# An opening and a last layer norm rebuilt in a two-layer encoder kernel: transfers in whole rows, a product on four column groups, rows of the last tile in PSUM

## The chip, the cores and the metric

The kernel runs on one core of a Trainium2 chip. The metric is the device time of one execution in microseconds (us), the median of several runs; less is better. The profile comes from one more execution, recorded by the hardware profiler.

## The reference, cut to what matters

256 tokens of width 1024 go through two layers. Each layer is a mixer (two kinds of heads side by side, one input projection, one output projection), a layer norm, a mixture of 16 experts with two experts for a token, and a second layer norm. All data is float32.

```python
def reference(x, ...):
    for i in range(2):
        mix = _even_mixer(x, ...) if i == 0 else _odd_mixer(x, ...)
        x = _layer_norm(ALPHA * x + mix, ln1_g[i], ln1_b[i])
        ffn = _hier_moe(x, ...)
        x = _layer_norm(ALPHA * x + ffn, ln2_g[i], ln2_b[i])
    return x

def _layer_norm(x, g, b):
    mu = mean(x); var = mean((x - mu) ** 2)
    return (x - mu) * rsqrt(var + 1e-5) * g + b

def _even_mixer(x, w_in, ...):
    h = x @ w_in
    z, xbc, dt_raw, q, k, v = split(h)
    dt = softplus(dt_raw + dt_bias)
...
```

## The kernel before, in words

One builder writes the instructions of all engines; the order of the program text is the order on each engine, and nothing is reordered. Weights come in pieces of 1 MB (128 partitions by 8 KB) into a ring of 19 buffers (`w`). `fill` (L163) issues their DMAs on SP's queue as soon as buffers come free.

**Opening** (`mixer0`, L305). Five small DMAs come first on SP's queue: `wdt` (the 16 columns of the first weight that give dt, 64 KB) and the transposed input `xT` in four pieces of 256 KB (rows of 2 KB in each partition). `load_constants` (L245) then issues the first weight buffer in two halves (rows of 4 KB), a second one, and constants (`pp`, `cc`, `cm`) between further weights. x is held as two float32r parts: ACT makes the high part `xh` (L319), DVE the rest `xl` (L320), in four pieces. PE meanwhile makes dt's product `dtp` (L339): eight matmuls of 16 columns from `xT` as it is, each recorded as two passes.

The main product of layer 0 goes over 32 pieces of 128 columns (loop at L548). `presplit` splits a piece of weights into high and low part (`split`, L222: ACT at L230, DVE at L231; tile `pair`), two pieces ahead. `mm3_stationary` (L234) then issues 8 matmuls high by `xh` (L238), 8 high by `xl` (L240) and 8 low by `xh` (L242). After a piece the convolution (L390, L393) or a copy takes its result off PSUM.

**Router constants.** After piece 14 the loop calls `router_prep(0)` (L843): six DVE operations add up the router's weights times the norm's gains (tile `rsum`, L852 to L855), one PE matmul (L857) adds over the partitions into `rbp`, and two DVE operations make `rbias` and the weights from it (L859, L860). For layer 1 `moe` (L863) calls it in its third quarter.

**End of a layer.** `moe` yields twice near its end; the code that follows takes it on with `next(moe)` (`mixer1` L1388 and L1389, `finale` L790). `combine` (L1082) adds an expert quarter into the PSUM banks `acc` of a token tile; the very last one is a float32 matmul of 512 columns (L1089). `residual_half` (L733) makes `xres` = ALPHA x + acc, `statistics` (L740) its sums, `moments` (L743) mean and a first root (two small ACT operations, L748 and L749), `factor` (L751) one Newton step on columns of 128x1 (L754 to L756), `shift` (L761) minus mean times factor.

`finale` writes the output. Tile 0 is scaled by ACT (L766) and gets gain and offset from POOL (L806, L807; stored from SP's queue, L808). Tile 1 is done by DVE: subtract the mean and times gain (L797), times factor plus offset (L799), a half at a time, second half first; L797 of the first of them stands ahead of `factor`. Its stores are issued from ACT's queue (L800). The gains and offsets `gb` lie in SBUF, as does `xres`.

Of the kernel before, what the change touches and what calls it, by code (L numbers as in the profile page):

```python
# [92 lines left out]
class Builder:  # L93
# [69 lines left out]
    def fill(self, n=1000, parts=1):  # L163
        while n and self.loaded < len(self.seq) and self.free > self.keep:
# [6 lines left out]
            for i in range(parts):  # L171
                cs = slice(n_el * i // parts, n_el * (i + 1) // parts)
                self.nc.sync.dma_start(w[:rows, cs], src[:, cs])
# [60 lines left out]
    def mm3_stationary(self, ps, hi, lo, xh, xl, n=8):  # L234

        mm = self.nc.tensor.matmul
        for c in range(n):
            mm(ps, hi[:, c, :], xh[:, c, :], start=(c == 0), stop=False)  # L238
        for c in range(n):
            mm(ps, hi[:, c, :], xl[:, c, :], start=False, stop=False)  # L240
        for c in range(n):
            mm(ps, lo[:, c, :], xh[:, c, :], start=False, stop=(c == n - 1))  # L242


    def load_constants(self):  # L245
        nc = self.nc
        nc.scalar.preload_act_table_set(EXP_LN)
        self.fill(1, 2)
        self.fill(1)
# [55 lines left out]
    def mixer0(self):  # L305
# [36 lines left out]
        dts = [self.T([128, 512], name="dts")]  # L342
        sc.activation(dts[0][:16, :256], dtp[:16, :256], AF.Copy)
# [196 lines left out]
        for i in range(32):  # L540
# [36 lines left out]
            if i == 16:  # L577
                self.reserve(4)
                self.gdone(2)
# [161 lines left out]

    def moments(self, t):
# [47 lines left out]
    def finale(self, gb, out, moe):  # L790
# [4 lines left out]
        def vector(t, s):  # L795
            x, mv = self.xres[:, t, HALVES[s]], self.mv[t]
            v.scalar_tensor_tensor(x, x, mv[:, 0:1], gb[:, 0, HALVES[s]], op0=OP.subtract, op1=OP.mult)  # L797
            yield
            v.scalar_tensor_tensor(x, x, mv[:, 3:4], gb[:, 1, HALVES[s]], op0=OP.mult, op1=OP.add)  # L799
            nc.scalar.dma_start(out[:, t, HALVES[s]], x)  # L800
            yield

# [7 lines left out]
        acc = next(moe)  # L810
        self.residual_half(1, 0, acc, stats=False)
        self.factor(0)
        self.shift(0)
        self.statistics(1, 0)
        self.residual_half(1, 1, acc)
# [992 lines left out]
```

## Time and profile before

| | |
|---|---|
| median of 3 runs | 526.71 us (526.57 to 528.31) |
| the profiled execution: its own time | 526.84 us |
| the profiled execution: span of the core | 525.0 us |
| mean granted TensorE clock | 0.992 |
| PE busy | 497.6 us, 95% |
| DVE, ACT, POOL busy | 301.6, 247.8, 94.1 us |
| DMA | 142.37 MB, mean 271 GB/s |

How to read it: the span runs from the first to the last recorded instruction; the execution's own time has 1.84 us more around it. PE's matmuls overlap one another, so the mean of one can be several times the distance between two. In a row of the timeline the first number is the start, the second the time from the first start to the last end of the instructions in it (x says how many); the bracket behind gives the engine's idle time before it and what ended it. Names such as `ps<-xh,pair` mean output from inputs.

### The profile page before, as it was taken

The page shows a single profiled execution, that of the slowest core. Times are in us where ns is not written, and L with a number is a line of the kernel's source. Part 1 is how long each engine was busy: PE and PEld are TensorE (multiplying, and loading weights), DVE is VectorE, ACT ScalarE, POOL GpSimd, SP SyncE. Part 2 cuts the span into 40 slices and gives each one's busy share as a digit, 9 for nine tenths or more (in the row PEclk, how much of TensorE's full clock was granted, in tenths as well). Part 3 has the DMA queues.
Part 4 walks back from the last instruction along what each step waited for, and adds up shares of the span by engine and source line. Part 5 has one row for each costly group of instructions (what it writes and reads, how often), then busy time and mean ns, then how long its engine had stood idle before and what let it go on. Part 6 is the DMA issues. An engine that isn't in the chain of part 4 may idle for free. (4 is left out here: it accounts for less than half of the span.)

```text
span 525.0 us, 9792 instructions
## 1 busy us (share of the span) xinstructions
PE 497.6 (95%) x3844; PEld 320.7 (61%) x3844; DVE 301.6 (57%) x683; ACT 247.8 (47%) x519; POOL 94.1 (18%) x161
## 2 busy tenths in 40 slices
PE   5999899999999999999999998999999999999990
PEld 2999898989777553433323698788776443533320
DVE  3777757777876762251206774887667741612047
ACT  4787467569783442240215583466644431512041
POOL 0073000120000002240002078910000002600204
PEclk9999999999999999999999999999999999999996
DMA  7999942006277969999979833070469699999602
GB/s 277 420 421 418 389 164 81 1 1 240 82 271 252 419 254 380 424 420 420 418 306 424 346 102 139 4 311 9 162 241 368 279 411 399 424 393 423 273 1 80
DMA packets 21179, 142.37 MB, mean 271 GB/s; under 512 B 2373, under 2 KB 2629, under 8 KB 4741
## 3 DMA queue, kind: packets, MB, share of 16 engines
q1 hardware_dynamic: 20024, 135.67, 64.5%
q0 software_dynamic: 816, 5.51, 2.8%
q8 instruction: 32, 0.52, 0.4%
q10 hardware_dynamic: 288, 0.52, 0.3%
q14 instruction: 19, 0.15, 0.1%
HBM read 140.64 MB, written 1.05 MB: 270 GB/s over the span
## 5 line engine op out<-in xcount | busy, mean ns | idle before, releaser
L1023 PE MATMUL gu<-w,XT 128*32 128x512 f32 x960 | 107.0, 594 | 0.0
L231 DVE TENSOR_TENSOR pair<-w,pair 128x1024 fp32r<-128x1024 f32 x57 | 70.3, 1236 | 25.0 <-ACT pair L230 24.6
L1023 PEld LDWEIGHTS gu<-w,XT 128*32 128x32 f32 x960 | 29.7, 110 | 65.4 <-issue 62.4
L230 ACT ACTIVATE pair<-w 128x1024 fp32r<-128x1024 f32 x57 | 60.2, 1060 | 8.8 <-PE ps L242 4.6
L1053 PE MATMUL dn<-w,hT 128*32 128x512 f32 x512 | 59.5, 596 | 0.9 <-ACT hT L1042 0.9
L1033 DVE TENSOR_TENSOR hd<-sg,gu 128x256 f32<-128x256 f32 x16 | 6.7, 420 | 78.6 <-ACT sg L1031 78.6
L238 PE MATMUL ps<-xh,pair 128*128 128x256 f32 x288 | 42.3, 289 | 1.4 <-ACT pair L230 1.4
L1072 DVE SCALAR_TENSOR_TENSOR pair<-dn,ws,pair 128x512 fp32r<-128x512 f32 x30 | 22.4, 749 | 35.2 <-ACT pair L1066 33.2
L240 PE MATMUL ps<-xl,pair 128*128 128x256 f32 x288 | 39.9, 281 | 0.0
L242 PE MATMUL ps<-xh,pair 128*128 128x256 f32 x288 | 39.8, 280 | 0.0
L1066 ACT ACTIVATE pair<-dn,ws 128x512 fp32r<-128x512 f32 x30 | 20.6, 687 | 37.7 <-PE dn L1053 29.9
L238 PEld LDWEIGHTS ps<-xh,pair 128*128 128x128 f32 x288 | 36.4, 189 | 2.9 <-ACT pair L230 1.9
L242 PEld LDWEIGHTS ps<-xh,pair 128*128 128x128 f32 x288 | 36.6, 188 | 0.0
L240 PEld LDWEIGHTS ps<-xl,pair 128*128 128x128 f32 x288 | 36.5, 188 | 0.0
L780 POOL PARTITION_BROADCAST w<-w x16 | 11.2, 798 | 136.7 <-DMA w<-in_ln_dram 86.5
L1031 ACT ACTIVATE sg<-gu 128x256 f32<-128x256 f32 x16 | 6.1, 381 | 62.5 <-PE gu L1023 62.5
L1053 PEld LDWEIGHTS dn<-w,hT 128*32 128x32 f32 x512 | 14.4, 109 | 30.4 <-issue 25.7
L993 ACT ACTIVATE XT<-gp,pp 128x256 f32<-128x256 f32 x36 | 17.6, 563 | 19.4 <-PE gp L986 19.4
L1549 ACT ACTIVATE pw<-z,sm 128x128 f32<-128x128 f32 (+1 forms) x32 | 13.0, 420 | 22.2 <-DVE sm L1546 9.9
L787 POOL TENSOR_TENSOR xres<-xres,w 128x256 f32<-128x256 f32 (+1 forms) x12 | 16.4, 1369 | 25.4 <-DVE hd L1033 12.7
L160 POOL DMA_DIRECT2D wh<-in_wgu_dram x4 | 2.3, 580 | 100.0 <-PE acc L685 100.0
L301 PE MATMUL vp<-pair,xh 128*128 128x256 f32 x128 | 19.8, 288 | 0.0
(370 smaller groups left out, 954.7 us busy)
## 6 DMA issues: line engine op xcount, KB each, us to landing
w<-in_wgu_dram SPq DMA_DIRECT2D x60, 1024.0 KB, 9.7
w<-in_wd_dram SPq DMA_DIRECT2D x32, 1024.0 KB, 11.3
w<-in_w_dram SPq DMA_DIRECT2D x15, 1024.0 KB, 17.1
w<-in_wout_dram SPq DMA_DIRECT2D x10, 1024.0 KB, 18.4
wh<-in_wgu_dram POOLq DMA_DIRECT2D x4, 1024.0 KB, 7.3
w<-in_wfox_dram SPq DMA_DIRECT2D x4, 1024.0 KB, 15.7
w<-in_wfv_dram SPq DMA_DIRECT2D x2, 1024.0 KB, 5.0
w<-in_wab_dram SPq DMA_DIRECT2D x2, 848.0 KB, 16.8
```

The lines of the kernel that those rows point to most:

```text
L230: self.nc.scalar.activation(vh, src, AF.Copy)
L231: (self.nc.gpsimd if pool else self.nc.vector).tensor_tensor(vl, src, vh.bitcast(F32), op=OP.subtract)
L238: mm(ps, hi[:, c, :], xh[:, c, :], start=(c == 0), stop=False)
L240: mm(ps, hi[:, c, :], xl[:, c, :], start=False, stop=False)
L242: mm(ps, lo[:, c, :], xh[:, c, :], start=False, stop=(c == n - 1))
L301: mm(o, xx[:, 4 * k + c, 128 * t:128 * t + 128], ww[:, c, :], start=(k == 0 and n == 0), stop=(k == 1 and n == 11))
L787: g.tensor_tensor(r, r, gb[:, 0, cs], op=OP.mult)
L993: sc.activation(xt[:, c, :], b[:, i], AF.Identity, bias=bb, scale=g)
L1023: pe.matmul(gu[t][32 * e:32 * e + 32, :], XT[t][:, c, o:o + 32], w[:, e, :], start=(c == 0), stop=(c == 7))
L1053: pe.matmul(b[32 * e:32 * e + 32, :], ht[:, k, 32 * e:32 * e + 32], w[:, e, :], start=(k == 0), stop=(k == 1))
L1066: sc.activation(y, dn[t, s], AF.Copy, scale=WS[t][:, q:q + 1])
L1072: v.scalar_tensor_tensor(yl, b, WS[t][:, q:q + 1], yh.bitcast(F32), op0=OP.mult, op1=OP.subtract)
```

## The change

1. `wdt` is padded to 32 columns for each of its 8 chunks (128 KB) and issued from ACT's queue, ahead of ACT's table load. `xT` comes in one DMA of 1 MB with rows of 8 KB, first on SP's queue. The first weight buffer comes in one DMA as well.
2. A tile of zeros (`idle`, bf16) feeds 8 matmuls of 512 columns ahead of dt's product, and 5 behind it; their result isn't used.
3. ACT makes pieces 0 and 1 of `xh`, DVE pieces 2 and 3, then all of `xl`.
4. dt's eight matmuls go to four groups of 32 columns of the array (partitions 0, 32, 64 and 96 of the output), two in each; a matmul with the constant `fold` later adds the four groups, in the place of two transposes.
5. For the first two pieces, the products with the high part of both stand ahead of those with the low part of both.
6. `router_prep` keeps the DVE sums; the matmul into `rbp` and what follows are `router_sums`, called after piece 16 (layer 0). In layer 1 the sums stand earlier, at the start of the third quarter.
7. In `factor` and `shift` the operations on 128x1 columns with two tensor inputs become TENSOR_SCALAR with one tensor input and two scalars from SBUF columns.
8. In `finale` tile 1's residual is added in place in PSUM; the last combine is two matmuls of 256 columns with an addition behind each; sums, mean and gain are taken from `acc`, and the last step writes to `xres`, which is stored from ACT's queue. `moe` therefore yields four times, in `mixer1` too.

```diff
-            for i in range(parts):
-                cs = slice(n_el * i // parts, n_el * (i + 1) // parts)
-                self.nc.sync.dma_start(w[:rows, cs], src[:, cs])
+            self.nc.sync.dma_start(w[:rows, :n_el], src)
...
         xT = self.G([128, 2048], name="xT")
-        wdt = self.T([128, 8, 16], name="wdt")
-        nc.sync.dma_start(wdt.rearrange("p c n -> p (c n)"), self.a["wdt"])
-        for i in range(4):
-            nc.sync.dma_start(xT[:, i * 512:(i + 1) * 512], self.a["xT"][:, i * 512:(i + 1) * 512])
+        wdt = self.T([128, 8, 32], name="wdt")
+        nc.scalar.dma_start(wdt.rearrange("p c n -> p (c n)"), self.a["wdt"])
+        nc.sync.dma_start(xT, self.a["xT"])
+
+        idle = self.T([128, 512], BF16, name="idle")
+        v.memset(idle, 0.0)
+        wu = self.B("wu")
+        for i in range(8):
+            pe.matmul(wu, idle[:, :128], idle, start=True, stop=True)
         xh = self.G([128, 8, 256], F32R, "xh")
         xl = self.G([128, 8, 256], F32R, "xl")
         xT3 = xT.rearrange("p (c t) -> p c t", c=8)
-        for i in range(4):
-            sc.activation(xh[:, 2 * i:2 * i + 2], xT3[:, 2 * i:2 * i + 2], AF.Copy)
-            v.tensor_sub(xl[:, 2 * i:2 * i + 2], xT3[:, 2 * i:2 * i + 2], xh[:, 2 * i:2 * i + 2].bitcast(F32))
+        chunks = [slice(2 * i, 2 * i + 2) for i in range(4)]
+        for i in (0, 1):
+            sc.activation(xh[:, chunks[i]], xT3[:, chunks[i]], AF.Copy)
+        for i in (2, 3):
+            v.tensor_copy(xh[:, chunks[i]], xT3[:, chunks[i]])
+        for cs in chunks:
+            v.tensor_sub(xl[:, cs], xT3[:, cs], xh[:, cs].bitcast(F32))
         pieces = {}
...
         dtp = self.B("dtp")
         for c in range(8):
-            pe.matmul(dtp[:16, :256], wdt[:, c, :], xT3[:, c, :], start=(c == 0), stop=(c == 7))
+            r = slice(32 * (c % 4), 32 * (c % 4) + 32)
+            pe.matmul(dtp[r, :256], wdt[:, c, :], xT3[:, c, :], start=(c < 4), stop=(c >= 4))
+        for i in range(5):
+            pe.matmul(wu, idle[:, :128], idle, start=True, stop=True)
+        del wu
         presplit(0)
         presplit(1)
...
             for t in range(2):
-                pe.transpose(dtt[:, 16 * t:16 * t + 16], d[:16, 128 * t:128 * t + 128], self.ident[:16, :16])
+                pe.matmul(dtt[:, 32 * t:32 * t + 32], d[:, 128 * t:128 * t + 128], self.cv("fold"), start=True, stop=True)
-            v.tensor_add(dt, dtt[:, :32].rearrange("p (t h) -> p t h", t=2),
+            v.tensor_add(dt, dtt[:, :64].rearrange("p (t h) -> p t h", t=2)[:, :, :16],
...
+            if i == 0:
+
+                ps2 = [self.A("ps")[:, :256] for _ in range(2)]
+                for k in range(2):
+                    self.mm3_stationary(ps2[k], *pieces[k], xh, xl, parts=(0, 1))
             presplit(i + 2)
             hi, lo = pieces.pop(i)
             ps = None
-            if i >= 28:
+            if i < 2:
+                ps = ps2[i]
+                self.mm3_stationary(ps, hi, lo, xh, xl, parts=(2,))
+            elif i >= 28:
...
             if i == 14:
                 self.router_prep(0)
             if i == 16:
+                self.router_sums(0)
                 self.reserve(4)
                 self.gdone(2)
...
-        v.scalar_tensor_tensor(mv[:, 6:7], mv[:, 5:6], mv[:, 5:6], mv[:, 2:3], op0=OP.mult, op1=OP.mult)
+        v.tensor_scalar(mv[:, 6:7], mv[:, 5:6], mv[:, 5:6], mv[:, 2:3], op0=OP.mult, op1=OP.mult)
-        v.tensor_mul(mv[:, 3:4], mv[:, 5:6], mv[:, 6:7])
+        v.tensor_scalar(mv[:, 3:4], mv[:, 6:7], mv[:, 5:6], None, op0=OP.mult)
-        v.scalar_tensor_tensor(mv[:, 4:5], mv[:, 0:1], -1.0, mv[:, 3:4], op0=OP.mult, op1=OP.mult)
+        v.tensor_scalar(mv[:, 4:5], mv[:, 0:1], mv[:, 3:4], -1.0, op0=OP.mult, op1=OP.mult)
...
+        def add(s, cs):
+            a = acc[s][:, cs]
+            v.scalar_tensor_tensor(a, self.xres[:, 1, HALVES[s]][:, cs], ALPHA, a, op0=OP.mult, op1=OP.add)
+
+
+        acc = next(moe)[1]
+        add(0, slice(0, 512))
         self.factor(0)
         self.shift(0)
-        self.statistics(1, 0)
-        self.residual_half(1, 1, acc)
         scalar(0, 0)
         scalar(0, 1)
+        for k in range(2):
+            next(moe)
+            add(1, slice(256 * k, 256 * k + 256))
+        self.st[1] = self.S([128, 2, 6], name="st", bufs=2)
+        for s in range(2):
+            v.bn_stats(self.st[1][:, s, :], acc[s])
         self.moments(1)
-        first = vector(1, 1)
-        next(first)
         self.factor(1)
-        next(first)
-        for _ in vector(1, 0):
-            pass
+        mv = self.mv[1]
+        for s in range(2):
+            a, cs = acc[s], HALVES[s]
+            x = self.xres[:, 1, cs]
+            v.scalar_tensor_tensor(a, a, mv[:, 0:1], gb[:, 0, cs], op0=OP.subtract, op1=OP.mult)
+            v.scalar_tensor_tensor(x, a, mv[:, 3:4], gb[:, 1, cs], op0=OP.mult, op1=OP.add)
+            nc.scalar.dma_start(out[:, 1, cs], x)
...
+    def router_sums(self, layer):
+
+        v, pe = self.nc.vector, self.nc.tensor
+        wr = self.wr
         rbp = self.B("rbp")
-        pe.matmul(rbp[:, :64], self.ones, u[:, :, 0], start=True, stop=True)
+        pe.matmul(rbp[:, :64], self.ones, self.rsum[:, :, 0], start=True, stop=True)
+        del self.rsum
         rbias = self.S([128, 24], name="rbias")
         v.tensor_add(rbias, rbp[:, :24], self.pv("rb", 24 * layer, 24))
...
             if last(q, t, s):
-                pe.matmul(acc[t][s], l.bitcast(F32), yy["last"], start=False, stop=True)
+                for c in (slice(256 * k, 256 * k + 256) for k in parts):
+                    pe.matmul(acc[t][s][:, c], l.bitcast(F32), yy["last"][:, c], start=False, stop=True,
+                              skip_group_check=True)
             else:
                 pe.matmul(acc[t][s], l, yh[:, cs], start=(q == 0), stop=False)
-                pe.matmul(acc[t][s], l, yl[:, cs], start=False, stop=(q == 3))
+                pe.matmul(acc[t][s], l, yl[:, cs], start=False, stop=(q == 3 or (q, t, s) == (2, 1, 1)))
...
         weigh_lo(3, 1, 1)
         combine(3, 1, 0)
-        combine(3, 1, 1)
         yield acc
+        for k in range(2):
+            combine(3, 1, 1, (k,))
+            yield acc
```

The order of the instructions at three places (a row is the line, the operation, output and inputs, the output's size, and in brackets the semaphores that it waits for). ACT's queue in the opening, before:

```order
L247 ACT_TABLE_LOAD
L319 ACTIVATE xh<-xT 128x512 [waits DMAHW1_49]
L319 ACTIVATE xh<-xT 128x512 [waits DMAHW2_49]
L319 ACTIVATE xh<-xT 128x512 [waits DMAHW3_49]
L319 ACTIVATE xh<-xT 128x512 [waits DMAHW4_49]
L230 ACTIVATE pair<-w 128x1024 [waits DMAHW5_49]
L230 ACTIVATE pair<-w 128x1024 [waits DMAHW6_49]
L343 ACTIVATE dts<-dtp 16x256 [waits PE_49]
```

And with the change:

```order
L311 DMA wdt<-in_wdt_dram 128x256
L248 ACT_TABLE_LOAD
L325 ACTIVATE xh<-xT 128x512 [waits DMAHW1_49]
L325 ACTIVATE xh<-xT 128x512
L228 ACTIVATE pair<-w 128x1024 [waits DMAHW2_49]
L228 ACTIVATE pair<-w 128x1024
L356 ACTIVATE dts<-dtp 128x256 [waits PE_49]
L228 ACTIVATE pair<-w 128x1024 [waits DMAHW3_49]
```

`wdt` is now issued here, two of the four splits of x are left, and both halves of the first weight wait for one DMA.

DVE around piece 16, from the last of the router's sums on (L855), before:

```order
L854 TENSOR_TENSOR rsum<-rsum 128x2x64 [waits DVE_49]
L855 TENSOR_TENSOR rsum<-rsum 128x2x32 [waits DVE_49]
L859 TENSOR_TENSOR rbias<-rbp,pp 128x24 [waits PE_49]
L860 SCALAR_TENSOR_TENSOR wrg<-rbp,wrg 128x256
L231 TENSOR_TENSOR pair<-w,pair 128x1024 [waits Activation_49]
L393 SCALAR_TENSOR_TENSOR cy<-ps,pp,cy 128x255 [waits Activation_49]
L393 SCALAR_TENSOR_TENSOR cy<-ps,pp,cy 128x254 [waits DVE_49]
```

And with the change, from the same operation (now L881) on:

```order
L881 TENSOR_TENSOR rsum<-rsum 128x2x32 [waits DVE_49]
L229 TENSOR_TENSOR pair<-w,pair 128x1024 [waits Activation_49]
L406 SCALAR_TENSOR_TENSOR cy<-ps,pp,cy 128x255 [waits Activation_49]
L406 SCALAR_TENSOR_TENSOR cy<-ps,pp,cy 128x254 [waits DVE_49]
L406 SCALAR_TENSOR_TENSOR cy<-ps,pp,cy 128x253 [waits DVE_49]
L229 TENSOR_TENSOR pair<-w,pair 128x1024 [waits DMAHW6_49,PE_49,Activation_49]
L891 TENSOR_TENSOR rbias<-rbp,pp 128x24 [waits PE_49]
L892 SCALAR_TENSOR_TENSOR wrg<-rbp,wrg 128x256
L229 TENSOR_TENSOR pair<-w,pair 128x1024 [waits Activation_49]
```

Between the last sum and the operation that waits for PE's `rbp` (L859, now L891) there now stand two splits of weights and the three operations of one convolution. On PE `rbp` moved likewise, behind the matmuls of two more pieces.

The end of the program: PE, before and with the change:

```order
L1053 MATMUL dn<-w,hT 32x512 [waits PE_49]
L1053 MATMUL dn<-w,hT 32x512 x7
L1091 MATMUL acc<-pair,PT 128x512 [waits Activation_49]
L1092 MATMUL acc<-pair,PT 128x512 [waits DVE_49]
L1089 MATMUL acc<-yl,PT 128x512 [waits Activation_49]
```

```order
L1085 MATMUL dn<-w,hT 32x512 x7
L1125 MATMUL acc<-pair,PT 128x512 [waits Activation_49]
L1126 MATMUL acc<-pair,PT 128x512 [waits DVE_49]
L1122 MATMUL acc<-yl,PT 128x256 [waits Activation_49]
L1122 MATMUL acc<-yl,PT 128x256 [waits DVE_49]
```

DVE from the first operation on the last half of the residual, before and with the change:

```order
L740 BN_STATS st<-xres 128x6
L733 SCALAR_TENSOR_TENSOR xres<-xres,acc 128x512 [waits PE_49]
L740 BN_STATS st<-xres 128x6 [waits DVE_49]
L746 BN_AGGR mv<-st 128x2 [waits DVE_49]
L747 TENSOR_SCALAR mv<-mv 128x1 [waits DVE_49]
L797 SCALAR_TENSOR_TENSOR xres<-xres,mv,w 128x512 [waits DMAHW4_49,Pool_49]
L754 SCALAR_TENSOR_TENSOR mv<-mv 128x1 [waits DVE_49,Activation_49]
L755 TENSOR_SCALAR mv<-mv 128x1 [waits DVE_49]
L756 TENSOR_TENSOR mv<-mv 128x1 [waits DVE_49]
L799 SCALAR_TENSOR_TENSOR xres<-xres,mv,w 128x512 [waits DVE_49,Pool_49]
L797 SCALAR_TENSOR_TENSOR xres<-xres,mv,w 128x512
L799 SCALAR_TENSOR_TENSOR xres<-xres,mv,w 128x512 [waits DVE_49]
```

```order
L827 SCALAR_TENSOR_TENSOR acc<-xres,acc 128x256 [waits PE_49] x2
L841 BN_STATS st<-acc 128x6
L841 BN_STATS st<-acc 128x6 [waits DVE_49]
L769 BN_AGGR mv<-st 128x2 [waits DVE_49]
L770 TENSOR_SCALAR mv<-mv 128x1 [waits DVE_49]
L777 TENSOR_SCALAR mv<-mv 128x1 [waits DVE_49,Activation_49]
L778 TENSOR_SCALAR mv<-mv 128x1 [waits DVE_49]
L779 TENSOR_SCALAR mv<-mv 128x1 [waits DVE_49]
L848 SCALAR_TENSOR_TENSOR acc<-acc,mv,w 128x512 [waits DMAHW0_49,Pool_49]
L849 SCALAR_TENSOR_TENSOR xres<-acc,mv,w 128x512 [waits DVE_49,Pool_49]
L848 SCALAR_TENSOR_TENSOR acc<-acc,mv,w 128x512
L849 SCALAR_TENSOR_TENSOR xres<-acc,mv,w 128x512 [waits DVE_49,Pool_49]
```

PE's last row now waits for DVE (the addition to the first 256 columns). On DVE the sums of both halves stand behind both additions, and no operation stands between the variance (L747, now L770) and `factor`.

## Rows read from the trace of the kernel before

**Rows 1.** The waits of PE: tile, line, releaser, us in total, times, longest.

```profile
PE rbp L857 <- DVE rsum L855: 1.7, 1, 1.7
```

**Rows 2.** The timeline of 0 to 14 us.

```profile
0.82 0.39 SPq L311 DMA_DIRECT2D wdt<-in_wdt_dram  x1
...
4.59 5.10 PE L339 MATMUL dtp<-xT,wdt 128*16 128x256 f32 x16 [4.59 <-DMA xT<-in_xT_dram]
5.14 0.69 DVE L320 TENSOR_TENSOR xl<-xT,xh 128x512 fp32r<-128x512 f32 x1 [5.14 <-ACT xh L319]
...
9.98 1.06 ACT L230 ACTIVATE pair<-w 128x1024 fp32r<-128x1024 f32 x1 [1.68 <-DMA w<-in_w_dram]
...
11.09 1.22 PE L238 MATMUL ps<-xh,pair 128*128 128x256 f32 x8 [1.40 <-ACT pair L230]
11.24 1.06 ACT L230 ACTIVATE pair<-w 128x1024 fp32r<-128x1024 f32 x1 [0.20 <-DMA w<-in_w_dram]
```

**Rows 3.** DMA issues by tile: KB each, median us from issue to landing.

```profile
w<-in_wfv_dram SPq DMA_DIRECT2D x2, 1024.0 KB, 5.0
```

**Rows 4.** Groups by line: busy us, mean ns, idle before them.

```profile
L1023 PE MATMUL gu<-w,XT 128*32 128x512 f32 x960 | 107.0, 594 | 0.0
...
L393 DVE SCALAR_TENSOR_TENSOR cy<-ps,pp,cy 128x255 f32<-128x255 f32 (+2 forms) x36 | 17.3, 480 | 2.0 <-ACT cy L390 1.1
```

**Rows 5.** Windows: PE, PEld, DVE, ACT, POOL busy, granted PEclk, DMA share, GB/s.

```profile
5.00:6.00 1.00, 1.00 (x4) 0.36 (x3) 0.69 (x1) 0.22 (x2) 0.00 (x0) 1.00 0.99 291
8.00:9.00 1.00, 1.00 (x6) 0.48 (x5) 1.00 (x2) 0.30 (x1) 0.00 (x0) 1.00 1.00 360
11.00:12.00 1.00, 0.91 (x7) 0.91 (x8) 0.93 (x1) 0.80 (x2) 0.00 (x0) 1.00 1.02 425
```

**Rows 6.** The timeline around the router's sums of layer 0.

```profile
56.35 1.11 PE L242 MATMUL ps<-xh,pair 128*128 128x256 f32 x8
...
59.20 0.43 PE L857 MATMUL rbp<-rsum,one 128*128 128x64 f32 x2 [1.74 <-DVE rsum L855]
...
60.10 1.21 DVE L231 TENSOR_TENSOR pair<-w,pair 128x1024 fp32r<-128x1024 f32 x1
```

**Rows 7.** The timeline of the end, tile 1.

```profile
511.37 1.13 PE L1089 MATMUL acc<-yl,PT 128*128 128x512 f32 x2
...
512.79 0.69 DVE L740 BATCH_NORM_STATS2 st<-xres 128x6 f32<-128x512 f32 x1
...
515.16 0.75 DVE L797 SCALAR_TENSOR_TENSOR xres<-xres,mv,w 128x512 f32<-128x512 f32 x1
...
515.83 1.22 DVE L754 SCALAR_TENSOR_TENSOR mv<-mv 128x1 f32<-128x1 f32 x1
517.00 1.25 POOL L806 TENSOR_TENSOR xres<-xres,w 128x512 f32<-128x512 f32 x1
...
517.09 0.15 DVE L755 TENSOR_SCALAR mv<-mv 128x1 f32<-128x1 f32 x1
517.27 1.00 DVE L756 TENSOR_TENSOR mv<-mv 128x1 f32<-128x1 f32 x1
...
518.37 1.77 DVE L799 SCALAR_TENSOR_TENSOR xres<-xres,mv,w 128x512 f32<-128x512 f32 x1
...
520.84 0.75 DVE L799 SCALAR_TENSOR_TENSOR xres<-xres,mv,w 128x512 f32<-128x512 f32 x1
```

**Rows 8.** The timeline at two places where DVE works beside POOL.

```profile
225.66 2.39 POOL L787 TENSOR_TENSOR xres<-xres,w 128x1024 f32<-128x1024 f32 x1 [1.30 <-ACT hT L1042]
227.51 0.75 DVE L1072 SCALAR_TENSOR_TENSOR pair<-dn,ws,pair 128x512 fp32r<-128x512 f32 x1 [1.34 <-ACT pair L1066]
...
331.06 0.29 DVE L1558 TENSOR_SCALAR pw<-pw,sm 128x128 f32<-128x128 f32 x1
331.26 0.89 DVE L1559 TENSOR_SCALAR pw<-pw,sm 128x256 f32<-128x256 f32 x1
331.27 0.73 POOL L788 TENSOR_TENSOR xres<-xres,w 128x256 f32<-128x256 f32 x1
```

More of the change, by code (lines that the diff above doesn't have):

```diff
@@ L161, in load_pair, with fill @@
         self.ring[i] = w
-    def fill(self, n=1000, parts=1):
+    def fill(self, n=1000):
         while n and self.loaded < len(self.seq) and self.free > self.keep:
@@ L232, in split, with mm3_stationary @@
         return vh, vl
-    def mm3_stationary(self, ps, hi, lo, xh, xl, n=8):
+    def mm3_stationary(self, ps, hi, lo, xh, xl, n=8, parts=(0, 1, 2)):
         mm = self.nc.tensor.matmul
[L237 to L242, printed above, removed]
+        if 0 in parts:
+            for c in range(n):
+                mm(ps, hi[:, c, :], xh[:, c, :], start=(c == 0), stop=False)
+        if 1 in parts:
+            for c in range(n):
+                mm(ps, hi[:, c, :], xl[:, c, :], start=False, stop=False)
+        if 2 in parts:
+            for c in range(n):
+                mm(ps, lo[:, c, :], xh[:, c, :], start=False, stop=(c == n - 1))
     def load_constants(self):
@@ L247, in load_constants @@
         nc.scalar.preload_act_table_set(EXP_LN)
-        self.fill(1, 2)
-        self.fill(1)
+        self.fill(2)
         self.pp = self.cp.tile([128, NPP], F32, name="pp")
@@ L338, in mixer0 @@
         for c in range(8):
-            pe.matmul(dtp[:16, :256], wdt[:, c, :], xT3[:, c, :], start=(c == 0), stop=(c == 7))
+            r = slice(32 * (c % 4), 32 * (c % 4) + 32)
[3 more added lines that the diff above has]
+        del wu
         presplit(0)
         presplit(1)
-        dts = [self.T([128, 512], name="dts")]
-        sc.activation(dts[0][:16, :256], dtp[:16, :256], AF.Copy)
+        dts = [self.T([128, 256], name="dts")]
+        sc.activation(dts[0], dtp[:, :256], AF.Copy)
         del dtp
@@ L793, in finale @@
         v, g = nc.vector, nc.gpsimd
[L795 to L801, printed above, removed]
         def scalar(t, s):
@@ L808, in scalar @@
             nc.sync.dma_start(out[:, t, HALVES[s]], x)
-        acc = next(moe)
-        self.residual_half(1, 0, acc, stats=False)
+        def add(s, cs):
[3 more added lines that the diff above has]
+        add(0, slice(0, 512))
         self.factor(0)
         self.shift(0)
-        self.statistics(1, 0)
-        self.residual_half(1, 1, acc)
         scalar(0, 0)
         scalar(0, 1)
+        for k in range(2):
[4 more added lines that the diff above has]
+            v.bn_stats(self.st[1][:, s, :], acc[s])
         self.moments(1)
-        first = vector(1, 1)
-        next(first)
         self.factor(1)
-        next(first)
-        for _ in vector(1, 0):
-            pass
+        mv = self.mv[1]
[5 more added lines that the diff above has]
+            nc.scalar.dma_start(out[:, 1, cs], x)
     def transposed(self, t, half):
@@ L843, in router_prep @@
     def router_prep(self, layer):
-        v, pe = self.nc.vector, self.nc.tensor
+        v = self.nc.vector
         n = 2 * layer
         wr = self.wr
-        u = self.T([128, 2, 8, 32], name="rsum")
+        self.rsum = u = self.T([128, 2, 8, 32], name="rsum")
         for k, name in enumerate(("lnb", "lng")):
@@ L1080, in down, with combine @@
             weigh_lo(q, t, s)
-        def combine(q, t, s):
+        def combine(q, t, s, parts=(0, 1)):
             yh, yl = yy[t]
@@ L1169, in moe @@
             if q == 2:
+                if layer == 0:
+                    self.router_prep(1)
                 gb = self.ln_rows(seq0 + 24)
@@ L1192, in moe @@
             if layer == 0 and q == 2:
-                self.router_prep(1)
+                self.router_sums(1)
             act(q, 1)
@@ L1387, in mixer1 @@
         krep = self.S([128, 2, 32], name="krep")
-        next(moe)
-        acc = next(moe)
+        for _ in range(4):
+            acc = next(moe)
         self.factor(0)
@@ L1775, in lay_out @@
     put("rb", np.broadcast_to(rb.reshape(48), (128, 48)))
-    o["wdt"] = f(dt.reshape(8, 128, 16).transpose(1, 0, 2).reshape(128, 128))
+    o["wdt"] = f(np.pad(dt.reshape(8, 128, 16).transpose(1, 0, 2), ((0, 0), (0, 0), (0, 16))).reshape(128, 256))
     wr = np.zeros((2, 1024, 32), np.float32)
```

## The prediction, made before the changed kernel had run

> **What bounds the kernel now.** The table of the profile says that PE is busy for nearly the whole span. Without less work for PE, what can be won is the time in which it stands still, and the work left after its last matmul. I read the waits of PE first: of those that the change touches, the router's sums cost 1.7 us, once [rows 1]. The timeline of the opening comes second: dt's matmuls start at 4.59 and end at 9.69, the first main matmul starts at 11.09, released by ACT's split of the first weight; that split started at 9.98, when half of the weight had landed [rows 2]. Pieces follow each other from there, so what PE gains at the start it keeps up to the sums. The timeline of the end comes third: PE's last matmul ends at 512.50, and DVE works on alone to 521.59 (520.84 + 0.75) [rows 7]; 3.4 us of store and end follow. So there are three places, each costed by itself. The sum is made against the profiled execution's 526.84 us, which is 0.13 above the median of the runs shown.
>
> **Opening.** The order of the transfers is now `xT` (1 MB, whole rows), then the first weight (1 MB), with `wdt` (128 KB) from ACT's queue beside them. The nearest row for 1 MB that meets idle DMA engines says 5.0 us from issue to landing [rows 3]. Issued at 0.82, as the first DMA was [rows 2], `xT` lands at 5.8; `wdt` takes its share of the engines, 0.13 MB at 425 GB/s [rows 5], so 6.1. The weight follows in the same queue: 1.05 MB is 2.9 us at the 360 GB/s of 8 to 9 us, while smaller rows moved, and 2.5 at the 425 of 11 to 12 us, with whole rows [rows 5]. I take 2.5, since the rows are whole now: 8.6. The split takes 1.06 [rows 2], and 0.05 to pass on: PE starts at 9.7, **1.4 us earlier**.
>
> Ready by then, and so costed at nothing:
> - dt's product. Matmuls of 32 columns on the four groups overlap already: 960 of 594 ns each make PE busy for 107.0 us, 0.11 each for 512 columns [rows 4]. Sixteen passes of 256 columns take 0.9 us, to 7.0; five idle matmuls of 512 columns at no more than 0.5 us each, twice the 0.25 of a pass of 256 columns in the window of 4 passes [rows 5], end by 9.5.
> - `xh` and `xl`: at most six DVE operations of 0.69 [rows 2] from 6.1, to 10.3. PE needs them one group of eight matmuls after 9.7, at 10.8.
> - DVE's first low part follows, to 11.5 (1.21 [rows 6]); with both high parts ahead, PE needs it after 32 matmuls, at 13.5.
>
> If that cover were gone, a low part would cost what it is late. Bounds: at 425 GB/s from 1.8 us on, 2.23 MB land at 7.1 and PE starts at 8.2, 2.9 earlier. If the first weight is whole only when its second half is now (ACT's second split, 11.24 [rows 2]), 1.06 of split and 0.2 for the added bytes make 12.5, 1.4 later. I stay nearest to the 1 MB row.
> The Trainium skill, "DMA: Bandwidth & Descriptors" (its two cost components, a fixed and a variable one), prices a transfer at about 2.0 us plus its bytes at 436 GB/s. For 1 MB that is an estimated 4.4 us where this trace has 5.0; by it PE would start at 9.1 and the forecast would read 521.8. The row decides.
>
> **Router sums, layer 0.** The last matmul ahead of them ended at 57.46 and `rbp` started at 59.20 [rows 6]: 1.74 us, all of it a wait for DVE's sums. With the change 48 matmuls of two more pieces, about 6.2 us at 0.13 each (7 in 0.91 [rows 5]), stand ahead of `rbp`, and the sums are long done. What is late next? The sums still hold up DVE: its low part for the piece after ran at 60.10 for 1.21 [rows 6], and without the wait for `rbp` it ends near 59.2 + 1.2 = 60.4. PE needs it 40 matmuls behind 57.46, at 62.7. DVE's own wait for `rbp` now stands two pieces on; behind it wait two short operations (under 0.5 each, as L393 [rows 4]) and a low part, 2.2 us together, which PE needs 40 matmuls (5.2 us) later. I take the whole **1.74**. Bounds: 0.9, if half of DVE's lateness returns at the next piece, and 1.74. In layer 1 PE has no such wait, so the move is worth nothing.
>
> **End.** Today `factor` starts at 515.83 and the operation behind it at 518.37: 2.54 us, of which L754 takes 1.22 and L756 1.00, the latter within POOL's L806. L755 between them, with one tensor input from SBUF, takes 0.15 beside the same L806 [rows 7]. The first L799 takes 1.77, the last 0.75. So the long ones have two tensor inputs from SBUF while POOL works. An operation with one from PSUM and one from SBUF took 0.75 with half of it inside POOL's L787 [rows 8]. From this:
> - Added ahead of the variance: at 512.79 DVE's scalars for tile 0 are done, and a sum, an addition and a sum follow, 3 x 0.69 [rows 7]. Now it is an addition of 256 columns (0.48, from L393 with 255 [rows 4]), PE's second half, which waits for it (half of 1.13, and 0.1 to pass on twice), the second addition (0.48) and two sums (1.38): 3.0 for 2.06, so 1.0 later.
> - `factor`: three operations 0.18 apart, as L755 to L756, 0.54 for 2.54. It starts at 516.83 and ends at 517.37.
> - L797, which stood at 515.16 while ACT made the root, moves behind `factor`: four operations of 0.75 stand there, to 520.37. Before: 521.59. **1.2 us earlier.**
>
> The stores go from ACT's queue as before. Bounds: 2.0 earlier if PE's second half is not held up, 1.8 later if `factor` stays stretched (+2.0) and one more operation does (+1.0).
> The Trainium skill, "SBUF — State Buffer" (Who interferes with whom), says that `tensor_scalar` can enter a mode that takes the ports which DVE shares with GpSimd, and that the one who comes first holds them for its whole instruction. By that rule the new `factor` could stay stretched. L755 speaks against it here, another row for it, so it is a rival below.
>
> **The rest, at nothing.** Layer 0's last combine is cut in two as well, with no addition between: 0.1 at most. Two matmuls with `fold` replace two transposes. `factor` and `shift` of the other norms save under 0.1 each.
>
> **Sum.** 526.84 − 1.4 − 1.74 − 1.2 = 522.5, less 0.13: **522.4 us**. With half of the bounds of opening and end its own range is 521.3 to 523.7. A measurement of this kernel can tell about 0.3%, 1.6 us, from no change: faster is below 525.1, slower above 528.3.
>
> **Rivals.**
> - The transfers run at 425 GB/s from the first packet on. For: the later window. Against: 5.0 us for 1 MB. 520.9, chance 0.10.
> - `factor` stays stretched. For: a TENSOR_SCALAR of 256 columns took 0.89 beside POOL's L788, one of 128 took 0.29 just before [rows 8]. Against: L755. 1.8 of the 2.0 us come back: 524.2, chance 0.07.
> - The opening edit does not do what it is made of: whole rows speed nothing, and waiting for the whole weight, 0.5 MB more, eats what the new order gives. PE starts at 11.1 as now: 523.8, chance 0.11.
> - The same, worse: `wdt` takes its share while `xT` should move, and the weight is whole no earlier than now. PE starts at 12.5: 525.2, within 0.3%, chance 0.12.
> - Slower: PE goes into the main product at a lower pace. dt's passes came 4 to a window at 5 us and 6 at 8 us, at a granted clock that reads 1.00 in both [rows 5]; PE had been idle until 4.59. Now it has idle matmuls first, then a stand until `xT` lands, then a shorter product. Each us of main matmuls at half pace costs 0.5 us: from 8.6 us on the gain of 4.3 is gone, from 11.8 on it is slower by over 0.3%. Against: 1.4 us of standing ahead of 11.09 did not slow the next eight (1.22) [rows 2]. 528.3 and more, chance 0.04.
>
> The forecast keeps 0.56. **Chances:** faster 0.56 + 0.10 + 0.07 + 0.11 = 0.84, within 0.3% 0.12, slower 0.04. **Range** 520.6 to 525.3: left out are the slower case, part of the full-rate case and the tails of the other bounds, between 0.15 and 0.2.
>
> **What would show it.** Right: the first split near 8.6 and the first main matmul near 9.7; no wait of PE for the router's sums; three operations of 0.15 in the last `factor`, four of 0.75 behind it, the last of them ending 6.5 us behind PE's last matmul (9.1 now); a wait of that matmul for DVE. Wrong: a first split after 10; a wait of PE for low parts after piece 14; a last `factor` over 1 us; main matmuls twice as far apart, or a granted clock below 1.00, after the start.

## The result: slower, and the profile after

Median 529.95 us (9 runs) against 526.71 for the kernel before; the ratio is 1.0057, 95% interval 1.0034 to 1.0079. Forecast was 522.4. The profiled execution took 529.08, its span is 527.3; that of before took 526.84, span 525.0.

The three places that the forecast costed came out nearly as costed. The opening, from the timeline of the changed kernel:

```profile
1.26 3.52 PE L319 MATMUL wu<-idle 128*128 128x512 bf16 x8 [1.26 <-DVE idle L316]
...
6.43 1.07 PE L349 MATMUL dtp<-xT,wdt 128*32 128x256 f32 x16 [1.65 <-DMA wdt<-in_wdt_dram]
...
7.43 1.25 PE L351 MATMUL wu<-idle 128*128 128x512 bf16 x5
8.71 2.01 ACT L228 ACTIVATE pair<-w 128x1024 fp32r<-128x1024 f32 x2 [1.34 <-DMA w<-in_w_dram]
...
9.82 1.22 PE L237 MATMUL ps<-xh,pair 128*128 128x256 f32 x8 [1.14 <-ACT pair L228]
```

The first split starts at 8.71 (forecast 8.6), the first main matmul at 9.82 (9.7; before 11.09 [rows 2]). The router's matmul has lost its stand, by the same view:

```profile
61.58 1.10 PE L243 MATMUL ps<-xh,pair 128*128 128x256 f32 x8
...
62.52 0.33 PE L888 MATMUL rbp<-rsum,one 128*128 128x64 f32 x2
```

There is no bracket behind L888 now, where [rows 6] has 1.74. I set equal matmuls of both traces side by side and took the difference of their starts: 1.27 us earlier at the first, 2.8 earlier at 80 us, still 2.3 earlier at 480 us. The end, from the timeline:

```profile
514.93 0.70 PE L1122 MATMUL acc<-yl,PT 128*128 128x256 f32 x2
...
516.52 0.42 DVE L827 SCALAR_TENSOR_TENSOR acc<-xres,acc 128x256 f32<-128x256 f32 x1
...
516.99 0.70 PE L1122 MATMUL acc<-yl,PT 128*128 128x256 f32 x2 [1.36 <-DVE acc L827]
...
520.29 0.27 DVE L777 TENSOR_SCALAR mv<-mv 128x1 f32<-128x1 f32 x1 [0.51 <-ACT mv L772]
520.60 0.15 DVE L778 TENSOR_SCALAR mv<-mv 128x1 f32<-128x1 f32 x1
520.79 0.21 DVE L779 TENSOR_SCALAR mv<-mv 128x1 f32<-128x1 f32 x1
520.92 0.75 DVE L848 SCALAR_TENSOR_TENSOR acc<-acc,mv,w 128x512 f32<-128x512 f32 x1
...
523.31 0.75 DVE L849 SCALAR_TENSOR_TENSOR xres<-acc,mv,w 128x512 f32<-128x512 f32 x1
```

`factor` is three operations of 0.27, 0.15 and 0.21 us (1.22, 0.15 and 1.00 before [rows 7]), and from the start of the last combine (514.93; 511.37 before) to DVE's last end (524.06; 521.59) it is 9.13 us for 10.22: 1.1 us less (forecast 1.2).

What is new stands between 480 and 494 us. `moe` has a conditional branch there (`overflow`, called at the end of the third quarter: a fallback for experts with more tokens than fit, hundreds of PE instructions, skipped with this input). The timeline of PE behind the branch, kernel before:

```profile
484.59 0.47 PE L1091 MATMUL acc<-pair,PT 128*128 128x512 f32 x1 [0.18 <-PEq L1249]
```

And the changed kernel (PEq is PE's own sequencer, "issue" a wait for nothing that the profile shows):

```profile
483.87 0.47 PE L1125 MATMUL acc<-pair,PT 128*128 128x512 f32 x1 [1.79 <-PEq L1287]
...
485.89 1.07 PE L1055 MATMUL gu<-w,XT 128*32 128x512 f32 x8
489.45 3.47 PE L1055 MATMUL gu<-w,XT 128*32 128x512 f32 x13 [2.49 <-issue]
```

PE stands for 1.79 us, runs 16 matmuls, stands for 2.49, and then 13 matmuls take 3.47 us. The windows of the changed kernel (columns as in [rows 5]) say why they are slow:

```profile
486.00:488.00 2.00, 0.95 (x8) 0.15 (x7) 0.00 (x0) 0.00 (x0) 0.00 (x0) 1.00 1.03 410
488.00:490.00 2.00, 0.55 (x4) 0.20 (x7) 0.00 (x0) 0.00 (x0) 0.00 (x0) 0.82 1.00 414
490.00:492.00 2.00, 2.00 (x13) 0.53 (x9) 0.00 (x0) 0.00 (x0) 0.00 (x0) 0.50 0.90 369
492.00:494.00 2.00, 2.00 (x20) 0.64 (x16) 0.00 (x0) 0.00 (x0) 1.39 (x3) 0.83 0.12 49
```

The granted clock is 0.50 there, the lower of TensorE's two levels (1.2 of 2.4 GHz), right after the stand. The PE that was 2.3 us ahead at 480 us is 3.6 behind at 495: this one place costs 5.9 us, more than everything else gains. No transfer of weights ends these waits: where one does, the view names it, and here it names the sequencer and "issue". DMA runs at 369 GB/s and more until 492 us, as it did in the kernel before.

### The profile page after: what moved, and what is told of

Its sections match the earlier page's. It is cut to its first block, busy times and chain, and to the rows that moved or that the text cites. A ratio compares the mean times of both kernels' runs of the same rounds, so it can differ in the third digit from the quotient of the medians.

```text
span 527.3 us, 9825 instructions
## 1 busy us (share of the span) xinstructions
PE 500.5 (95%) x3863; PEld 322.4 (61%) x3863; DVE 300.6 (57%) x687; ACT 246.2 (47%) x517; POOL 93.7 (18%) x161
## 3 DMA queue, kind: packets, MB, share of 16 engines
HBM read 140.71 MB, written 1.05 MB: 269 GB/s over the span
## 5 line engine op out<-in xcount | busy, mean ns | idle before, releaser
L1055 PE MATMUL gu<-w,XT 128*32 128x512 f32 x960 | 108.8, 601 | 2.5 <-issue 2.5
```

The costliest lines, as they stand in the source:

```text
L1055: pe.matmul(gu[t][32 * e:32 * e + 32, :], XT[t][:, c, o:o + 32], w[:, e, :], start=(c == 0), stop=(c == 7))
```

## The experiments

The theory after this: PE's instructions come from memory in blocks, the trace records their transfers as a DMA queue of kind "instruction", and behind a jump the stand depends on where the jump's target lies in its block. The change put 26 PE instructions (13 idle matmuls with their weight loads) ahead of everything. The number of packets of that queue from 480 to 492 us, from the DMA view, is 2 in the kernel before:

```profile
q8 instruction: 2, 0.03, 1.1%
```

and 3 in the changed one:

```profile
q8 instruction: 3, 0.05, 1.7%
```

The count alone is no sign of a stand: two runs below have 2 in this window and a stand of 1.8 us all the same. When a packet starts tells more; that comes behind the table of stands.

The rivals: PE comes to the branch too early for something else, the idle matmuls harm in another way, or another part of the change does. Ratios below are to the kernel before, run on the same chip beside them.

**Without the idle matmuls.** Edit on the changed kernel:

```diff
-        for i in range(8):
-            pe.matmul(wu, idle[:, :128], idle, start=True, stop=True)
-        for i in range(5):
-            pe.matmul(wu, idle[:, :128], idle, start=True, stop=True)
```

> The changed kernel without its 13 idle matmuls (26 PE instructions fewer ahead of everything else; all else as changed). Theory: the loss sits behind the conditional branch of layer 1 (PE stands 1.8 and 2.5 us there and its matmuls then run at half pace for 3.3 us, 1.6 us more), because the instructions behind the branch's target cross into a block that PE's sequencer has not fetched yet; where that crossing lies depends only on the number of PE instructions ahead. Then taking 26 away moves the crossing by 26 instructions, the stand goes or becomes much shorter, and the time falls to about 523 to 524. Rival: PE comes to the branch 2.5 us earlier than before and finds something not ready (weights, the DMA engines full): then nothing changes here, 529 to 530. Second rival, for the opening alone: without idle matmuls the first main matmuls run at half pace, up to 1.5 us later at the start.

0.9949 (0.9924 to 0.9974). PE's timeline has the branch as in the kernel before:

```profile
485.75 0.47 PE L1117 MATMUL acc<-pair,PT 128*128 128x512 f32 x1 [0.18 <-PEq L1279]
```

The second rival for the opening is right as well, and larger than I had it. PE's timeline:

```profile
9.79 2.08 PE L237 MATMUL ps<-xh,pair 128*128 128x256 f32 x8 [1.46 <-ACT pair L228]
...
16.28 2.04 PE L243 MATMUL ps<-xh,pair 128*128 128x256 f32 x16
```

Eight matmuls take 2.08 us instead of 1.22, and the normal pace comes back at 15.6 us only. At the trace position of 25.75 us PE is 2.4 us behind the changed kernel. So in these two profiles the idle matmuls are worth 2.4 us in the opening and cost 5.9 at the branch.

**Only the idle matmuls, in the kernel before.** The same lines added, nothing else.

> The kernel before with the 13 idle matmuls and their tile of zeros, and nothing else of the change (26 PE instructions more ahead of the branch; they stand where PE waits anyhow, 8 ahead of dt's product and 5 behind it). Theory (place of the crossing behind the branch): a stand of 2 to 4 us and half-pace matmuls behind the branch appear though no other part of the change is there: 529 to 532. Rival (PE comes too early, or another part of the change): no stand, 526.5 to 527.

1.0116 (1.0085 to 1.0147). PE's timeline:

```profile
486.56 0.47 PE L1099 MATMUL acc<-pair,PT 128*128 128x512 f32 x1 [3.54 <-PEq L1257]
```

A stand of 3.54, and the window of 488 to 490 us has a granted clock of 0.52. So no other part of the change is needed for it.

**More idle matmuls.** 24 small ones ahead of dt's product (48 PE instructions), then 12 (24):

```diff
+        for i in range(24):
+            pe.matmul(wu[:32, :32], idle[:, :32], idle[:, :32], start=True, stop=True)
```

> The changed kernel with 24 more, small idle matmuls (32 by 32) in the opening, while PE waits for the input: 48 PE instructions more ahead of the branch, no work else. Theory: about 34 instructions ran behind the branch's target before PE stood, so 48 more put the target itself behind the crossing, with most of a block ahead of it: the stand is gone, 522 to 524. Rival (PE too early at the branch): unchanged, 529 to 530.

0.9944 (0.9922 to 0.9965): the same kernel with 24 useless matmuls added goes from slower to faster than the one before. PE's timeline:

```profile
482.61 0.47 PE L1127 MATMUL acc<-pair,PT 128*128 128x512 f32 x1 [0.39 <-PEq L1289]
```

> As the run with 24 small idle matmuls, but with 12 (24 PE instructions more). Theory: the crossing now comes about 10 instructions behind the target, so PE still stands behind the branch, after fewer of its matmuls: 528 to 532, with fewer matmuls between the branch and the stand. Rival: unchanged, the stand after the same 8 matmuls of the gate product, 529 to 530.

0.9962 (0.9941 to 0.9983), faster than both had it; one stand of 1.77 at the branch itself, no second one, no half pace. So the time and the place were a miss.

**The kernel before with the same numbers.** 13 idle and 24 small matmuls, later 36 and 26:

> The kernel before with the 13 idle matmuls and the 24 small ones: 74 PE instructions more ahead of the branch, and no other part of the change. Theory (place of the block crossing behind the branch): the stand that 26 more gave (3.5 us, half-pace matmuls behind it) is gone: within 0.3% of the kernel before. Rival (idle matmuls in the kernel before do harm in another way): 531 to 535 as with 13.

1.0058 (1.003 to 1.0086): a miss. Its stand at the branch is 1.80 us. Another loss of 1.5 us stands behind the router's sums: the 1.74 us wait is there as in [rows 6], and in this execution the clock fell behind it. Windows of this run:

```profile
59.00:61.00 2.00, 1.84 (x15) 1.84 (x16) 1.47 (x4) 0.00 (x0) 0.00 (x0) 0.95 1.01 422
61.00:63.00 2.00, 2.00 (x11) 2.00 (x11) 1.63 (x4) 0.00 (x0) 0.00 (x0) 0.50 1.01 422
```

> The kernel before with 13 idle matmuls and 36 small ones, 98 PE instructions more ahead of the branch (the run with 24 small ones had 74, and a stand of 1.8 us). Theory: behind the place where the stand goes, it is gone, as in the changed kernel with 78 more than before: within 0.3% of the kernel before. Rival (idle matmuls harm the kernel before in another way): 0.5% slower as with 24.

1.0109 (1.0076 to 1.0142), a miss, and a telling one: at layer 1's branch nothing is lost, but the branch of **layer 0** now has a stand of 2.22 us and a second of 2.4, which with the half pace behind them cost 6.1 us. The profiled execution (538.0, the slowest of five) loses 1.6 us more behind the router's sums and 3.5 at a wait of PE for DVE; the clock fell behind both.

> The kernel before with 13 idle matmuls and 26 small ones: 78 PE instructions more, as many as in the changed kernel with 24 small ones. Theory: no stand behind either branch; 526.5 to 528, within 0.3% of the kernel before, so that the rest of the change is worth the whole of the 0.5% that the changed kernel with 24 small ones gains. Rival (idle matmuls do harm in the kernel before in some other way): 0.5% and more slower, as with 24 and 36 small ones.

1.0031 (1.0004 to 1.0058): no stand in layer 0, 1.67 us in layer 1 without half pace behind it. Neither theory nor rival as written. My count was off here: at the branch of layer 1 the changed kernel with 24 small ones has 82 more and not 78, since the cut combine of layer 0 adds four.

**One block more.** 64 small idle matmuls ahead of dt's product and 64 behind, 256 PE instructions.

> The changed kernel with 128 small idle matmuls (256 PE instructions) more ahead of the branch, half of them ahead of dt's product and half behind it. The trace records PE's instruction fetches as packets of 16384 bytes; at 64 bytes for an instruction one of them is 256 instructions, which is an estimate of mine from the distance at which the stand came and went. Theory (the stand hangs on where the branch's target lies in such a block): one whole block more brings the changed kernel's stand back as it was, about 1.8 us at the branch and some 2.5 us eight gate matmuls later; the opening may be 1 to 2 us longer. Rival (it is the number of instructions as such, or chance): no stand or one elsewhere, as with 48 more.

1.0098 (1.0063 to 1.0133), from two executions. The stand is back at layer 1's branch, 2.91 us and a second of 0.8, with half pace between them; from 480 to 495 us PE loses 5.3 us (5.9 in the changed kernel). Another 2.3 us were lost at a wait of PE for DVE near 455 us.

**Parts of the end and of the opening**, each on the kernel with 24 small idle matmuls. First the last combine whole, with one addition behind it:

```diff
-                for c in (slice(256 * k, 256 * k + 256) for k in parts):
+                for c in [slice(0, 512)][:1 - parts[0]]:
...
-            add(1, slice(256 * k, 256 * k + 256))
+            if k == 0:
+                add(1, slice(0, 512))
```

> The run with 24 small idle matmuls, with the last combine as one matmul of 512 columns again and one addition behind it (in both layers; 4 PE instructions fewer ahead of the branch of layer 1). Theory for the end: cutting it costs time, because PE's second half waited 1.36 us for DVE's addition to the first half, which itself waits for DVE's scalars of tile 0; whole, the matmul ends at about 1.1 us behind its start, DVE's single addition (0.69) starts right behind the scalars as the first half's does now, and the sums start some 0.85 us earlier: 0.7 to 0.9 us less than the run with 24 small idle matmuls. Rival: the halves let the addition overlap with the matmul, so whole is 0.3 to 0.5 slower.

0.9954 (0.9929 to 0.9979). The time alone can't tell, since the opening and the branch came out 0.9 us worse in this profile: 0.6 at the start, 0.6 more at the branch, 0.3 less between. The timeline of the end can. From the last combine's start:

```profile
510.28 1.13 PE L1125 MATMUL acc<-yl,PT 128*128 128x512 f32 x2
...
517.68 0.75 DVE L852 SCALAR_TENSOR_TENSOR xres<-acc,mv,w 128x512 f32<-128x512 f32 x1
```

8.15 us, where the same stretch with halves is 9.11 (509.41 to 518.52) in the run it is built on. Cutting the combine costs 0.96.

Then `factor` with its two old operations:

```diff
-        v.tensor_scalar(mv[:, 6:7], mv[:, 5:6], mv[:, 5:6], mv[:, 2:3], ...)
+        v.scalar_tensor_tensor(mv[:, 6:7], mv[:, 5:6], mv[:, 5:6], mv[:, 2:3], ...)
-        v.tensor_scalar(mv[:, 3:4], mv[:, 6:7], mv[:, 5:6], None, op0=OP.mult)
+        v.tensor_mul(mv[:, 3:4], mv[:, 5:6], mv[:, 6:7])
```

> The run with 24 small idle matmuls, with the two operations of `factor` on 128x1 columns that had two tensor inputs (SCALAR_TENSOR_TENSOR and TENSOR_TENSOR) put back. Theory: beside POOL's work on tile 0 they take about 1 us each again instead of 0.27 and 0.21, and the end is 1.5 to 2 us longer. Rival (they were stretched only by what L797 and L799 did before): 0.2 to 0.3 each, no change.

0.9972 (0.9939 to 1.0004). DVE's timeline, with POOL beside it:

```profile
514.77 1.20 DVE L779 SCALAR_TENSOR_TENSOR mv<-mv 128x1 f32<-128x1 f32 x1 [0.50 <-ACT mv L774]
516.00 0.15 DVE L780 TENSOR_SCALAR mv<-mv 128x1 f32<-128x1 f32 x1
516.03 1.26 POOL L824 TENSOR_TENSOR xres<-xres,w 128x512 f32<-128x512 f32 x1
516.19 1.12 DVE L781 TENSOR_TENSOR mv<-mv 128x1 f32<-128x1 f32 x1
```

1.20 and 1.12 again, as the theory had it. POOL belongs to it: on tile 0 of the same run, ahead of POOL's work, the same two take 0.21 and 0.16 (at 510.24 and 510.67 us).

Then the first weight in two DMAs (`fill` with its old `parts`):

```diff
-        self.fill(2)
+        self.fill(1, 2)
+        self.fill(1)
```

> The run with 24 small idle matmuls, with the first weight in two DMAs of half its columns (rows of 4 KB) again, the input still in one. If the first split waits for bytes alone, half the weight lands 1.0 to 1.2 us earlier and the first main matmul starts at 8.7 to 9.0 in place of 9.74: 0.7 to 1.0 us less. Rival (rows of 4 KB move slower, or the idle matmuls behind dt's product, which end at 8.6, hold PE): 0.3 less at most, or slower.

0.9923 (0.9896 to 0.9951). The timeline:

```profile
8.19 1.06 ACT L230 ACTIVATE pair<-w 128x1024 fp32r<-128x1024 f32 x1 [0.73 <-DMA w<-in_w_dram]
...
9.29 1.20 PE L239 MATMUL ps<-xh,pair 128*128 128x256 f32 x8 [0.54 <-ACT pair L230]
```

PE starts 0.45 us earlier (9.74 in the run it is built on): between theory and rival. Half the weight comes 0.44 us ahead of the whole, not 1.0.

**All that helps, together.** Whole combine, halves of the weight, 36 small idle matmuls, then 26:

> The changed kernel with three things that the runs so far point to: 36 small idle matmuls (72 PE instructions more ahead of the branch, less 4), the last combine as one matmul, the first weight in two DMAs. Theory: the gains add up, since they lie at the start, behind the branch and at the end: 1.0 us less than the run with the weight in halves for the whole combine, so 522 to 523 where that one had 523.3, 0.990 of the kernel before. Rival: the stand behind the branch comes back at this number of instructions: 525 and more.

1.003 (0.9999 to 1.006), a miss by the same cause at the other branch. PE's timeline in layer 0:

```profile
255.09 0.47 PE L1131 MATMUL acc<-pair,PT 128*128 128x512 f32 x1 [2.01 <-PEq L1293]
...
257.11 1.06 PE L1061 MATMUL gu<-w,XT 128*32 128x512 f32 x7
260.75 1.93 PE L1061 MATMUL gu<-w,XT 128*32 128x512 f32 x8 [2.58 <-issue]
```

The same picture as in the changed kernel, at the other branch.

> As the run with three changes at once, but with 26 small idle matmuls in the place of 36: 78 PE instructions more ahead of the branches than in the kernel before. The run with 36 (98 more) had its stand behind the branch of layer 0, and those with 78 more had none or 0.5 us behind either. Theory (the number of PE instructions ahead decides): no stand behind either branch, the gains of the whole combine (1.0) and of the weight in halves (0.5 to 0.7) add to those of the run with 24 small ones: about 522, 0.990 of the kernel before. Rival (the stand hangs on the whole combine or the halves themselves): a stand again, 526 and more.

0.9911 (0.9877 to 0.9945), 522.64 us where the kernel before had 527.68: faster than both kernels. It differs from the run ahead of it by ten idle matmuls of 32 by 32 alone.

The stands by the number of PE instructions ahead of each branch (matmuls and weight loads of the traces), more than in the kernel before. The changed kernel has four more from the product with `fold`, and four more ahead of layer 1's branch from the cut combine of layer 0. Each row is one profiled execution:

| more, layer 0 / 1 | kernel | stand, layer 0 | stand, layer 1 | ratio |
|---|---|---|---|---|
| 0 / 0 | before | 0.18 | 0.18 | 1 |
| 4 / 8 | changed, no idle | 0.18 | 0.18 | 0.9949 |
| 26 / 26 | before, 13 idle | 0.18 | 3.54 | 1.0116 |
| 30 / 34 | changed | 0.18 | 1.79 + 2.49 | 1.0057 |
| 54 / 58 | changed, 12 small | 0.18 | 1.77 | 0.9962 |
| 74 / 74 | before, 24 small | 0.18 | 1.80 | 1.0058 |
| 78 / 78 | before, 26 small | 0.18 | 1.67 | 1.0031 |
| 78 / 78 | whole combine | 0.18 | 0.99 | 0.9954 |
| 78 / 82 | changed, 24 small | 0.18 | 0.39 | 0.9944 |
| 78 / 82 | old factor | 0.18 | 0.33 | 0.9972 |
| 78 / 82 | weight in halves | 0.18 | 0.55 | 0.9923 |
| 82 / 82 | all three, 26 small | 0.18 | 0.67 | 0.9911 |
| 98 / 98 | before, 36 small | 2.22 + 2.4 | 0.18 | 1.0109 |
| 102 / 102 | all three, 36 small | 2.01 + 2.58 | 0.18 | 1.003 |
| 286 / 290 | changed, 256 more | 0.18 | 2.91 + 0.8 | 1.0098 |

The trace has the start of every instruction packet, and these times say more than the numbers ahead. Four of the stands (us):

| kernel | packet starts | PE stands from | PE goes on |
|---|---|---|---|
| changed | 481.21 | 482.08 | 483.87 |
| changed, 24 small | 479.90 | 482.23 | 482.61 |
| before, 13 idle | 483.90 | 483.02 | 486.56 |
| before, 26 small | 482.86 | 483.91 | 485.57 |

In all 13 stands at a branch PE goes on 2.66 to 2.80 us after the start of a packet; at the 17 crossings with nothing lost (0.18), the last packet had started 3.49 us or more before PE went on. The second stands end 2.35 to 2.49 us after the start of the next packet. So the length of a stand is what is left of about 2.7 us when PE comes to the branch. The period is in these times too: with 256 instructions more there is one packet more near the start (at 11.18 us), and the next ones start at 18.62, 33.51 and 49.51 where the changed kernel's start at 18.60, 33.37 and 49.26.

Shown: idle instructions ahead, with nothing else changed, make and remove the stands, and a stand ends about 2.7 us after the start of an instruction packet. That PE waits for the block which this packet brings is the reading that fits all 30 crossings; the profile has no event that names it. The Trainium skill, "Runtime: NRT & Kernel Launch" (Instruction fetch mechanics), says that instructions come in blocks of 16 KiB, 256 instructions, and that a taken branch to a target outside the blocks at hand waits for a transfer; the period found here agrees. Open is what sets the start of the packet: it is 1.05 us ahead of the stand at 78 more in the kernel before and 2.33 at 82 more in the changed one. Both kernels also carry a branch hint for each of the two branches (`hint`); no run leaves it out, so its part isn't shown.

## Why the prediction was wrong

- **Opening, −1.4:** right; −1.27 measured. The 1 MB input took 5.4 us from issue to landing (0.82 to 6.22), nearer to the row's 5.0 than to the 4.4 by the price of the Trainium skill that the prediction names; its page gives that price as a fit for transfers issued from GpSimd, and here SP issued.
- **Router sums, −1.74:** right about the stand, which is gone; by 80 us the gain of both terms is 2.8 where 3.1 was forecast. PE waits 0.3 us for POOL before the decay rows now.
- **End, −1.2:** right; 1.1 measured. Its parts hold too: the old `factor` costs 1.8 us (1.20 + 1.12 for 0.27 + 0.21), and the cut combine costs 0.96, costed at 1.0. I took that term as given by the change and did not ask whether its place should be left out; whole, the end would have gained 2.1.
- **"Ready by then, and so costed at nothing", the failing step:** the 13 idle matmuls were costed by their duration beside the waits in the opening, and as time they are indeed covered. What they move is the program: 26 instructions ahead of two branches, so that an instruction packet starts 0.87 us before PE comes to the second one. The stands and the half pace at the second branch cost 5.9 us (−2.3 to +3.6), where the sum had no term at all. The same matmuls are worth 2.4 us in the opening, which the sum also left out, having put the pace into a rival. The sum counted PE's waits for data alone and had no wait of PE for its own instructions.
- **"Pieces follow each other from there, so what PE gains at the start it keeps":** kept to 480 us within 0.5 us, and lost at the branch.
- **The slower rival, 0.04:** that the kernel came out slower is no hit for it. The mechanism of half pace is real (eight matmuls in 2.08 us without idle matmuls; a granted clock of 0.50 after stands) but not at the place where I put it, and too small there to make the kernel slower. Its evidence was misread as well: the 1.00 of the windows at 5 us [rows 5] is no measurement, since that trace's first record of the clock starts at 7.65 us, just where dt's passes go from 0.43 us apart to 0.21. That PE's sequencer can itself be late was no case of mine: "PEq L1249", 0.2 us, was in the waits of PE of the kernel before.
- **The stretched `factor`, 0.07:** refuted; 0.27, 0.15 and 0.21 beside POOL.
- **The narrower range, 521.3 to 523.7:** half of the bounds of opening and end gives 525.3 at its upper end, which is the top of the range that I stated; 529.95 lies outside either. The parts of the additions ahead of the variance add up to 3.1 us, not 3.0, which changes nothing.

In sum: −1.27, −1.5, +0.5 over the middle, +5.9 and −1.1 make +2.5; the spans differ by 2.3.

## What to carry to other kernels

An edit that costs no time can still shift an engine's whole program, and behind a jump that shift can cost several us; when a change is slower than its parts, set equal instructions of both traces side by side and look where the difference jumps, before doubting the parts, and then at the starts of the instruction packets ahead of that place. In a kernel with branches, try a change with a few tens of idle instructions more or less ahead before judging it. An in-place step that is cut to overlap two engines gains only if the second engine is free at once; here it was busy, and the cut cost a wait.

## What the runs showed that I had not expected

- A stand of PE can cost as much again: the granted clock read 0.50 for 3.4 us behind the branch wherever the stands came to 2.9 us and more (five profiles), and not behind single stands of 1.67 to 1.80 (three). Behind the router's wait of 1.7 to 1.8 us it fell in two profiles (1.5 us lost in the first) and not in three, that of the kernel before among them.
- Without work ahead of them, main matmuls run at half pace for 5.8 us at the start, while the granted clock in the rows reads 1.00. That 1.00 is no measurement: the trace's first record of the clock starts at 15.62 us, and the matmuls go from 0.21 us apart to 0.12 just there, which fits the lower of the two levels until then. In the changed kernel the first record starts at 4.57. The same idle matmuls don't always do it: in three other profiles with them it starts at 9.8 to 10.6. The window without idle matmuls, 10 matmuls in 2 us:

```profile
10.00:12.00 2.00, 2.00 (x10) 2.00 (x11) 2.00 (x2) 1.71 (x3) 0.00 (x0) 1.00 1.01 403
```

  and the same window of the changed kernel, 18:

```profile
10.00:12.00 2.00, 2.00 (x18) 2.00 (x19) 2.00 (x2) 1.73 (x3) 0.00 (x0) 1.00 0.99 395
```

- Splitting the first weight again, which the change gave up, is 0.45 us faster at the start.
